# Differential attention: an odd key tile's value product first, the even one queued right behind it

## The chip, the cores and the metric

The kernel runs on one core of one Trainium2 chip. The metric is device time in microseconds (us) of one execution. A program of this kind has one instruction stream for each engine: TensorE (PE, its weight loads are listed as PEld), VectorE (DVE), ScalarE (ACT), GpSimd (POOL) and SyncE (SP, which issues most transfers). Each stream is worked off in its order, and the engines wait for one another by semaphores.

## The reference

A two-layer diffusion transformer block on 256 context tokens and 1024 latent tokens, width 1024. Each layer mixes tokens in three groups of heads (RWKV-7, differential attention, windowed attention), projects the result and runs a gated MLP. What the change touches is the differential attention: four heads, two softmax maps for each, and one product of their difference with the values.

```python
def diff_core(q, k, v, lam):
    s = jnp.einsum('bqhmd,bkhmd->bhmqk', q, k, preferred_element_type=F32) * (DF_QK ** -0.5)
    p = jax.nn.softmax(s, axis=-1)
    p = p[:, :, 0] - lam * p[:, :, 1]
    return jnp.einsum('bhqk,bkhd->bqhd', p.astype(v.dtype), v)
```

## The kernel before

`run` (line 2046) goes through the two layers. In a layer come, one after the other but overlapping at their borders: the input projection, token mixing, the output projection and the MLP. Token mixing is the RWKV scan (`rw_rest`, 20 steps, each a chain of small products) with the differential attention beside it, and then the windowed attention (`gq_units`, line 1439). All arithmetic is float32.

The differential attention (`df_units`, line 1299) is made of units, one for each head and group of query blocks: layer 0 has three groups for each head (256 context queries, then twice 512 latent queries), layer 1 the two latent ones. A unit has two generators. `scores` (line 1334) takes the scores once with the queries on the partitions, for their maxima and sums (lines 1356, 1369, 1371, 1349), and writes minus the maximum as further rows of the queries (`max_rows`, line 1207). `values` (line 1393) takes the scores again with a tile of 128 keys on the partitions, for each of the two maps (line 1412), exponentiates them into a tile `p` on ScalarE (line 1413), forms the difference of the maps in place on VectorE (line 1418), and multiplies by the values on TensorE (line 1425).

That value product has a stationary operand of 128 keys by 64 channels. Key tiles of even number add up in rows 0 to 63 of the accumulator `o`, those of odd number in rows 64 to 127; `result` (line 1400) copies `o` out on ScalarE (line 1402), adds the halves by a product with `fold` (line 1405) and finishes the head. A latent unit has ten key tiles, so five pairs; a context unit two, so one pair. That makes 84 pairs in all: 44 in layer 0 and 40 in layer 1. One product of 512 queries is two records in the trace (two passes over float32 operands).

Buffers that matter: `p` has three (`PTB`), the score banks `ds` in PSUM two (`XB`; the second scores, the first scores, the modulation's products `ada` and the folding share them), the accumulator `od` one (`ODB`), keys `ks` and values `vh` of a head one each.

What sets the order: the two products of a pair are emitted together by `product`, which is put on the list `late` and emitted one pair late (`flush`, `DLD`). `streams` (line 1234) interleaves the scores of later units with the values of earlier ones by their costs, and `blend` adds the modulation of the next half layer (`ada`, line 284). The emission order is only a priority. A planner then fixes the order of each engine's stream before the run, from its own estimate of when each instruction's operands are ready; the differential attention is emitted after the RWKV scan, with its priority raised over up to 4000 (layer 0) or 1000 (layer 1) earlier instructions (`HPO`). An even tile's `p` is ready before the odd tile's, and nothing ties the two products of a pair together in TensorE's stream.

Of the kernel before, what the change touches and what calls it, by code (L numbers as in the profile page):

```python
# [17 lines left out]
PSUM = bass.MemoryType.PSUM  # L18
DRAM = bass.MemoryType.DRAM

D = 1024
T = 1280
# [134 lines left out]
class K:  # L157
# [16 lines left out]
    def sbuf(self, name, tags=(), side="left"):  # L174
        """open an SBUF pool for these tags (all that have no pool of their own if none are given)"""
        es = ExitStack()
        p = es.enter_context(self.tc.tile_pool(name=name, bufs=1, reuse_waits="tile", side=side))
        for t in tags:
            self.pools[t] = p
            es.callback(self.pools.pop, t)  # L180
        if not tags:
            self.mp = p
        return es

    def psum(self, name, banks, side="left"):
        """open a PSUM pool; banks: use (None: any other) -> (tag, number of banks)"""
        es = ExitStack()
        self.pp = p = es.enter_context(self.tc.tile_pool(name=name, bufs=1, space=PSUM, reuse_waits="tile", side=side))
        for n, (t, k) in banks.items():
            self.banks[n] = (p, t, k)  # L190
            es.callback(self.banks.pop, n, None)
        return es
# [4 lines left out]
    def sm(self, shape, tag, bufs=2, dt=F32):  # L197
        """small tile that outlives a phase"""
# [13 lines left out]
    def rsqrt(self, y, ss, scale, eps, n, op1=ALU.add, tag="n"):  # L212
        """y = (ss*scale op1 eps)^-1/2 on [128, n]; Newton from a bit estimate."""
# [20 lines left out]
    def split(self, hi, lo, src, eh, el):  # L234
        """hi + lo = src exactly (both float32r)."""
# [17 lines left out]
    def consts(self):  # L253
# [7 lines left out]
        # split queries, keys (feature-major, hi and lo rows per head) and values (token-major)  # L261
# [9 lines left out]
        # silu(c), silu(c_ctx), feature-major  # L271
# [12 lines left out]
    def ada(self, l, chunks, bufs):  # L284
        """silu(c) @ ada_w + ada_b by chunks of 256 columns, gates times their norm_g -> DRAM; a chunk's quarters
        side by side in the array's column groups"""
# [28 lines left out]
    def ada_first(self):  # L315
        """shift and scale of layer 0's mixing, feature-major: as modT gives them"""
# [30 lines left out]
    def modT(self, l, part):  # L347
        """A = norm_g*(1+sc), SH, feature-major [128, 2(x, ctx), 8]."""
# [17 lines left out]
    def params(self, l):  # L366
        """per-channel parameters, feature-major"""
# [18 lines left out]
    def rw_consts(self, l):  # L386
# [8 lines left out]
        # lora weights, block-diagonal over the directions: rows of w_up, then of a_up  # L395
# [53 lines left out]
    def xsrc(self, i, t):  # L449
        """DRAM rows of token tile t of the stream after step i (i = -1: inputs)."""  # L450
# [9 lines left out]
    def norm_rows(self, src, tiles):  # L460
        """rows of these token tiles, normalized"""
# [20 lines left out]
    def norm_steps(self, src, tiles, A, SH, dst, one=None, hb=HB):  # L482
        """dst(k) -> (hi, lo) APs of the columns of these token tiles (only column `one` if given)."""
# [16 lines left out]
    # token tiles of the two halves of each group  # L500
# [15 lines left out]
    def wchunk(self, l, cols):  # L516
        """Split weight pieces of w_in[l] for the 8 row blocks; cols: [(first, width)]."""
# [17 lines left out]
    def fm_proj(self, W, o, m, evac, g, halves):  # L535
        """feature-major projection to columns o..o+m of chunk W over the tokens of group g's halves"""
# [8 lines left out]
    def rw_proj(self, W, o, j, g, halves):  # L545
        """raw projection of channel tile j (r0 r1 k0 k1 v0 v1) -> DRAM"""
# [25 lines left out]
    def tm_proj(self, W, i, j, w):  # L572
        """token-major projection of tile j of half i"""
# [6 lines left out]
    def rope(self, dst, ps, tab, g, dim):  # L580
        """dst = rope(ps), ps [128, g*dim]; tab [128, 2*dim] = cos | signed sin."""
# [16 lines left out]
    def parts(self, x, src, n, w, d, scale=1.0):  # L598
        """x [128, 2*w] = hi and lo values of scale*src's n groups of d columns, side by side per group"""
# [8 lines left out]
    def stacks(self, x, n):  # L608
        """[128, n, 128]: the n [128, 128] tiles of x transposed"""
# [14 lines left out]
    # (first output column, columns of w_in) of the chunks of the attention projections  # L624
    ATTN = ((0, [(960, 512)]), (512, [(1472, 256), (2240, 256)]), (1024, [(1728, 512)]))

    def attn_proj(self, l, g, W0=None, done=None):
        """q, k, v of both attentions (q and k split) -> DRAM"""
# [3 lines left out]
        for base, cols in self.ATTN:  # L632
            W = W0 if W0 and base == 0 else self.wchunk(l, cols)
            for i, j, t in [(i, j, t) for i in range(2) for j, t in enumerate(self.GROUPS[g][i])]:
# [28 lines left out]
                def store(base=base, t=t, x=x, tok=tok):  # L663
                    if base == 0:
                        st = self.stacks(x, 8).rearrange("p (a h) t -> p a h t", a=2)
                        # queries as high, high, low rows; keys as high, low, high rows
# [21 lines left out]
    def in_rwkv(self, l, g):  # L688
        """projections of the RWKV group"""
# [16 lines left out]
    def in_weights(self, l):  # L706
        """the first chunk's weights, in slots that the FFN is done with"""
# [14 lines left out]
    def in_first(self, l, src, done):  # L722
        """group 0"""
# [21 lines left out]
    # Both channel tiles (two heads each) run side by side. Index u of a step's matrices is  # L745
    # (direction, channel tile, head). Steps are prepared in batches; BATCH lists each batch's steps.
    BATCH = ((0, 1, 2, 3), (4, 5, 6, 7, 16, 17, 18, 19), (8, 9, 10, 11, 12, 13, 14, 15))

    def rw_conv(self, ct, pr, v, last, x):
        """width-3 convolution of r, k, v of one channel tile over 256 tokens; v goes to its tile"""  # L750
# [31 lines left out]
    def rw_prep(self, st, ct, pr, last, x=""):  # L782
        """Chunk operands of both directions for a 256-token piece of one channel tile (two heads).

        Direction 1 runs on reversed tokens: its storage index is T-1-token."""
# [16 lines left out]
        # normalised kk  # L802
# [7 lines left out]
        # decay: cumulative log decay of the chunk, inclusive and exclusive  # L810
# [20 lines left out]
        # in-context rate  # L831
# [56 lines left out]
    def chunk(d, s):  # L888
        """storage chunk of step s (context first in both directions)"""
        return s if d == 0 else (16 + s if s < 4 else s - 4)  # L890

    def rw_system(self, st, ct, b, p0):
        """the unit-triangular systems of four steps of batch b (from its position p0) -> DRAM"""
# [18 lines left out]
    def rw_inverse(self, b):  # L912
        """inverses of the batch's 32x32 diagonal blocks -> DRAM, as they are and transposed"""
# [24 lines left out]
    def rw_gram(self, st, s):  # L938
        """masked Gram matrices of step s; the systems' quadrant holds the inverses"""
# [33 lines left out]
    def rw_kv(self, st, s):  # L973
        """token-major keys (times the decay of the rest of the step) and values of step s"""
# [22 lines left out]
    def rw_step(self, st, s, last):  # L997
# [7 lines left out]
        # rows 0..63: outputs, rows 64..127: right sides of the systems  # L1005
# [59 lines left out]
    def rw_readout(self, st, tiles, tag="rt", bufs=6, end=False):  # L1065
        """group norm, bonus, output gate of two token tiles -> scr_y"""
# [43 lines left out]
    def sooner(self, g, offset):  # L1110
        """a generator whose instructions go before up to `offset` earlier ones"""
# [8 lines left out]
    def together(*gs):  # L1120
        """run generators side by side"""
# [9 lines left out]
    def beside(*gs):  # L1131
        """one generator that runs these side by side"""
# [12 lines left out]
    def rw_first(self, l, last):  # L1145
        """what the first steps need"""
# [46 lines left out]
    # Scores are taken twice: with queries on the partitions, for their maxima, and with keys on the  # L1193
    # partitions and minus the maximum as further rows of the product, for the exponentials, which are
    # then the moving operand of the product with [V | 1].
# [3 lines left out]
    def cast(self, out, in_):  # L1199
        """load split values (exact)"""  # L1200
        self.nc.gpsimd.dma_start(out=out, in_=in_)

    def ones(self, k, r):
        """the rows of the keys that meet the maxima"""
        self.nc.gpsimd.memset(k[r:r + 8].bitcast(F32), 1.0)

    def max_rows(self, q, r, nm, n, mask, bank="mT"):
        """rows r..r+8 of q [128, n*128]: for column block b, nm[:, b]'s high part in row b and low part in row 4+b"""
# [12 lines left out]
    def unflip(self, o, n, d, tag, bank="yT"):  # L1221
        """[128 rows, n, d] PSUM view of o [d, n*128] PSUM, transposed"""
# [11 lines left out]
    def streams(self, units, late, lead, ahead):  # L1234
        """units: (scores, values, their costs), generators that yield costs; the values run beside the scores of
        up to `lead` units further on, both streams at the same share of their total costs. A unit's last entry is the
        number of units whose values have to be done before its scores. Yields costs too."""
# [22 lines left out]
    def blend(*gs):  # L1260
        """run generators (with their total costs) side by side, at the same share of the costs"""
# [10 lines left out]
    def limit(g, cost):  # L1272
        """the part of a generator up to a cost"""
# [8 lines left out]
    def flush(late, n):  # L1282
        """emit the products with the values but for the latest n"""
# [3 lines left out]
    def neg_log(self, y, L, n):  # L1287
        """y = -ln(L) on [128, n] for L >= 1: estimate from the bits, then Newton steps on exp"""
# [10 lines left out]
    def df_units(self, l, late):  # L1299
        """differential attention: units of a head for up to four row blocks"""  # L1300
# [5 lines left out]
        for hd in range(DF_HEADS):  # L1306
# [23 lines left out]
            for gi, (t0, nt) in enumerate(groups):  # L1330
# [3 lines left out]
                def scores(t0=t0, nt=nt, nk=nk, us=us, hs=hs, first=gi == 0, head=head, hd=hd):  # L1334
# [7 lines left out]
                    # maxima and sums of the context keys (0) and of the other keys (1)  # L1342
# [4 lines left out]
                    def chunk(c, m, i, s):  # L1347
                        """exponentials' sum of chunk c, component m, row block i"""
# [44 lines left out]
                def values(t0=t0, nt=nt, nk=nk, us=us, hs=hs, finish=finish):  # L1393
# [14 lines left out]
                    for j in range(nk):  # L1408
# [13 lines left out]
                        def product(pair=tuple(pair)):  # L1422
                            for j, p in pair:
                                r = 64 * (j % 2)
                                mm(o[r:r + 64, :w], v[:, j], p[:, 0, :w], start=j < 2, stop=j >= nk - 2)
# [13 lines left out]
    def gq_units(self, l, late):  # L1439
        """windowed attention: units of the four heads of a key group at one row block"""  # L1440
# [5 lines left out]
        for qt, g in ((qt, g) for qt in range(t1, NT) for g in range(2)):  # L1446
# [23 lines left out]
            def scores(g=g, qt=qt, kts=kts, us=us, hs=hs, head=head):  # L1470
# [14 lines left out]
                def prod(o, h, k0, n):  # L1485
                    """scores of head h against n keys from tile k0"""
# [75 lines left out]
    def post(self, y, ss, rs, gate, x, out, junk):  # L1562
        """out = x + y*rsqrt(mean y^2)*gate for y given as two [128, 512] halves"""
# [589 lines left out]
```

## Time and profile before

| | us |
|---|---|
| median of 3 runs | 4740.43 |
| lowest and highest run | 4727.01, 4759.02 |
| span of the profiled execution | 4717.0 |
| TensorE busy in it | 4264.7 (90%) |
| VectorE, GpSimd, ScalarE busy | 3238.9 (69%), 2324.3 (49%), 1861.2 (39%) |

The span runs from the first to the last instruction of one profiled execution, a separate one from the three timed runs. Its own time outside the span is not recorded, so the three runs are the only whole times. Busy time of TensorE counts from the start of a product to its modelled end, so products that follow each other closely overlap in it.

The value products stand in eight stretches of the span, four for each layer (one for each head): 556 to 628, 768 to 823, 964 to 1032 and 1201 to 1301 us in layer 0; 2975 to 3036, 3156 to 3200, 3344 to 3391 and 3555 to 3636 us in layer 1. The last stretch of each layer lies beside the windowed attention, the others beside the RWKV scan.

### The profile page before, as it was taken

What the parts mean: (1) busy time and instruction counts of PE and PEld (TensorE: products, weight loads), DVE (VectorE), ACT (ScalarE), POOL (GpSimd) and SP (SyncE); (2) the same over time, 40 slices, a digit from 0 to 9 for tenths busy, and PEclk for the clock granted to TensorE, in tenths of its full rate; (3) what the DMA queues carried; (4) which work ended last, traced back from release to release, by engine and by line L of the source; (5) the groups of instructions that cost most, each with busy time, mean ns of one, the idle gap of its engine ahead of it and who ended that gap; (6) DMA issues with size and microseconds to landing.
All of it is one profiled execution on the core that took longest, in us unless ns stands there. A gap on an engine that the chain in (4) does not pass through costs nothing. (4 is left out here: it accounts for less than half of the span.)

```text
span 4717.0 us, 71390 instructions
## 1 busy us (share of the span) xinstructions
PE 4264.7 (90%) x25999; PEld 3353.6 (71%) x25999; DVE 3238.9 (69%) x6313; ACT 1861.2 (39%) x3692; POOL 2324.3 (49%) x2295
## 2 busy tenths in 40 slices
PE   8997998989998999889988989889899989897897
PEld 5885664845567899779977866457555678886886
DVE  4347666777756877887774366656776478888887
ACT  3334544534333333433333344555443233333332
POOL 3336225243445666576654252542534366667664
PEclk9996868977999999999999985789879889998998
DMA  7453223251132222232235461222510322223222
GB/s 211 127 144 94 63 71 95 60 149 57 29 128 94 87 83 83 88 113 81 81 106 163 121 149 27 72 56 68 130 49 29 114 95 90 85 90 99 86 89 85
DMA packets 500637, 441.20 MB, mean 94 GB/s; under 512 B 120372, under 2 KB 432828, under 8 KB 500286
## 3 DMA queue, kind: packets, MB, share of 16 engines
q1 hardware_dynamic: 447070, 381.44, 27.1%
q0 software_dynamic: 21056, 51.26, 4.1%
q10 hardware_dynamic: 32160, 3.94, 0.5%
q8 instruction: 205, 3.36, 0.3%
q14 instruction: 146, 1.20, 0.1%
HBM read 353.02 MB, written 83.51 MB: 93 GB/s over the span
## 5 line engine op out<-in xcount | busy, mean ns | idle before, releaser
L244 DVE TENSOR_TENSOR wl<-wraw,fwh 128x1024 fp32r<-128x1024 f32 x176 | 324.1, 1842 | 160.4 <-ACT fwh L238 159.8
L238 ACT ACTIVATE fwh<-wraw 128x1024 fp32r<-128x1024 f32 x264 | 272.2, 1053 | 301.7 <-DVE wraw L1854 169.0
L248 PE MATMUL m<-h,fwh 128*128 128x322 f32 (+1 forms) x1056 | 320.7, 304 | 15.4 <-ACT fu L1900 8.6
L248 PE MATMUL dn<-dh,ahl 128*128 128x512 f32 x792 | 315.9, 403 | 14.9 <-ACT ahl L238 9.3
L244 POOL TENSOR_TENSOR gp<-gx,gp 128x512 fp32r<-128x512 f32 x160 | 207.5, 1301 | 246.0 <-DVE gp L240 166.8
L249 PE MATMUL dn<-dl,ahl 128*128 128x512 f32 x792 | 319.4, 403 | 8.6 <-POOL dl L244 8.6
L250 PE MATMUL m<-h,wl 128*128 128x322 f32 (+1 forms) x1056 | 318.6, 302 | 4.3 <-DVE wl L244 4.3
L249 PE MATMUL m<-h,fwh 128*128 128x322 f32 (+1 forms) x1056 | 321.0, 304 | 0.0
L244 POOL TENSOR_TENSOR dl<-dr,dh 128x1024 fp32r<-128x1024 f32 x88 | 218.8, 2486 | 200.1 <-ACT dh L238 197.8
L250 PE MATMUL dn<-dh,ahl 128*128 128x512 f32 x792 | 305.4, 400 | 0.0
L1349 ACT ACTIVATE ds<-ds,dnm 128x512 f32<-128x512 f32 (+1 forms) x400 | 232.3, 581 | 185.0 <-DVE dnm L1371 106.9
L248 PE MATMUL m<-T,fwh 128*128 128x322 f32 (+1 forms) x704 | 222.2, 316 | 88.2 <-DVE fraw L1871 76.3
L244 POOL TENSOR_TENSOR wl<-wraw,fwh 128x1024 fp32r<-128x1024 f32 x88 | 230.1, 2615 | 123.0 <-ACT fwh L238 118.8
L1413 ACT ACTIVATE p<-ds 128x512 f32<-128x512 f32 (+1 forms) x336 | 187.4, 585 | 234.2 <-PE ds L1412 201.5
L1962 DVE TENSOR_TENSOR yacc<-dn,yacc 128x512 f32<-128x512 f32 x360 | 231.0, 680 | 26.4 <-PE dn L250 26.3
L244 POOL TENSOR_TENSOR ahl<-cv,ahl 128x642 fp32r<-128x642 f32 (+1 forms) x88 | 131.8, 1498 | 233.0 <-ACT ahl L238 214.0
L1930 ACT ACTIVATE cv<-cv 128x642 f32<-128x642 f32 (+1 forms) x88 | 60.5, 687 | 467.6 <-DVE cv L1929 467.6
L1371 DVE TENSOR_REDUCE dnm<-ds 128x1 f32<-128x512 f32 x256 | 173.9, 686 | 87.6 <-PE ds L1369 86.1
L244 DVE TENSOR_TENSOR wl<-wr,wh 128x512 fp32r<-128x512 f32 (+1 forms) x76 | 66.6, 879 | 239.5 <-ACT wh L238 136.7
L250 PE MATMUL m<-T,wl 128*128 128x322 f32 (+1 forms) x704 | 217.1, 308 | 8.6 <-DVE wl L244 8.6
L249 PE MATMUL m<-T,fwh 128*128 128x322 f32 (+1 forms) x704 | 218.7, 311 | 1.3 <-DVE T L244 1.2
L248 PEld LDWEIGHTS m<-h,fwh 128*128 128x128 f32 x1056 | 205.0, 194 | 19.9 <-ACT fu L1900 9.8
(499 smaller groups left out, 13524.0 us busy)
## 6 DMA issues: line engine op xcount, KB each, us to landing
wraw<-in_ff_w_gate_dram SPq DMA_DIRECT2D x88, 512.0 KB
wraw<-in_ff_w_up_dram SPq DMA_DIRECT2D x88, 512.0 KB
dr<-in_ff_w_down_dram SPq DMA_DIRECT2D x88, 512.0 KB
aw<-in_ada_w_dram SPq DMA_DIRECT2D x160, 256.0 KB
wr<-in_w_in_dram SPq DMA_DIRECT2D x88, 256.0 KB
x<-scr_x SPq DMA_DIRECT2D x28, 512.0 KB
scr_df<-st SPq DMA_DIRECT2D x80, 128.0 KB
scr_gq<-st SPq DMA_DIRECT2D x18, 512.0 KB
```

Of the source, the lines that this page charges most:

```text
L238: nc.scalar.activation(hi, src, AF.Copy)
L244: e.tensor_tensor(out=lo, in0=src, in1=hi, op=ALU.subtract)
L248: mm(out, lh, rh, start=first, stop=False)
L249: mm(out, lh, rl, start=False, stop=False)
L250: mm(out, ll, rh, start=False, stop=last)
L1349: act.activation(s, s, AF.Exp, bias=nm[:, c, m, i:i + 1], accum_out=L[:, c, m, i:i + 1])
L1371: vv.tensor_reduce(out=nm[:, 1 + c, m, i:i + 1], in_=s, axis=AX.X, op=ALU.max, negate=True)
L1413: act.activation(p[:, m, :w], s[:, :w], AF.Exp)
L1930: act.activation(t[:, m], t[:, m], AF.Silu)
L1962: vv.tensor_tensor(out=ys[i][:, hs], in0=ps, in1=ys[i][:, hs], op=ALU.add)
```

## The change

Inside `product`, the odd tile's product is emitted first. The even tile's product follows inside `issue_after`, which adds an edge without a semaphore: in TensorE's own stream the even product may only stand behind the odd one. The rows of `o` that each writes, the operands, and the first and last flags stay as they were.

```diff
                         def product(pair=tuple(pair)):
-                            for j, p in pair:
-                                r = 64 * (j % 2)
-                                mm(o[r:r + 64, :w], v[:, j], p[:, 0, :w], start=j < 2, stop=j >= nk - 2)
+
+                            (j0, p0), (j1, p1) = pair
+                            i1 = mm(o[64:128, :w], v[:, j1], p1[:, 0, :w], start=j1 < 2, stop=j1 >= nk - 2)
+                            with self.tc.issue_after(i1.ins):
+                                mm(o[0:64, :w], v[:, j0], p0[:, 0, :w], start=j0 < 2, stop=j0 >= nk - 2)
+                            j = j1
                             if j == nk - 1:
                                 result()
```

The rest of the diff removes comments and docstrings.

## Rows read from the trace of the kernel before

**Rows 1.** The page: the span, and TensorE's busy time, share and instructions.

```profile
span 4717.0 us, 71390 instructions
PE 4264.7 (90%) x25999; PEld 3353.6 (71%) x25999; DVE 3238.9 (69%) x6313; ACT 1861.2 (39%) x3692; POOL 2324.3 (49%) x2295
```

**Rows 2.** Busy time by stretch: line 1425 alone, TensorE and its weight loads, clock.

```profile
556.00:628.00 72.00, 27.65 (x44) 4.62 (x44) 0.82 0.28 80
768.00:823.00 55.00, 21.84 (x44) 4.03 (x44) 0.93 0.45 132
964.00:1032.00 68.00, 22.62 (x44) 4.05 (x44) 0.80 0.67 171
1201.00:1301.00 100.00, 22.10 (x44) 4.02 (x44) 1.00 0.11 29
2975.00:3036.00 61.00, 25.44 (x40) 4.49 (x40) 0.81 0.28 77
3156.00:3200.00 44.00, 23.10 (x40) 4.19 (x40) 0.90 0.36 104
3344.00:3391.00 47.00, 20.14 (x40) 3.73 (x40) 0.96 0.54 139
3555.00:3636.00 81.00, 20.16 (x40) 3.72 (x40) 1.00 0.08 23
sum 528.00, PE 183.04 PEld 32.85; mean PE 22.88 PEld 4.11
```

**Rows 3.** TensorE's timeline: products of line 1425 by themselves (start, length, idle before).

```profile
560.85 1.07 PE L1425 MATMUL od<-p,vh 128*64 128x512 f32 x2
...
585.44 1.97 PE L1425 MATMUL od<-p,vh 128*64 128x512 f32 x2
...
780.48 1.07 PE L1425 MATMUL od<-p,vh 128*64 128x512 f32 x2
781.48 0.73 PE L1412 MATMUL ds<-qs,ks 104*128 104x512 f32 x2
782.14 1.07 PE L1425 MATMUL od<-p,vh 128*64 128x512 f32 x2
...
3634.81 1.07 PE L1425 MATMUL od<-p,vh 128*64 128x512 f32 x2
```

**Rows 4.** The same timeline: two products of a pair side by side, x4.

```profile
625.06 1.97 PE L1425 MATMUL od<-p,vh 128*64 128x512 f32 x4
...
990.86 1.08 PE L1425 MATMUL od<-p,vh 128*64 128x512 f32 x4
```

**Rows 5.** Line 1425 by itself: its weight loads (shortest, median, longest in ns).

```profile
L1425 PEld LDWEIGHTS od<-p,vh x336: 132/136/232, 556.1 to 3634.9; 128*64 128x64 f32 x168
```

**Rows 6.** All engines by stretch: TensorE, weight loads, VectorE, ScalarE, GpSimd, clock.

```profile
556.00:628.00 72.00, 65.62 (x397) 31.03 (x398) 61.51 (x192) 36.04 (x70) 19.71 (x27) 0.82 0.28 80
768.00:823.00 55.00, 49.41 (x430) 22.45 (x431) 29.90 (x70) 26.19 (x48) 39.30 (x65) 0.93 0.45 132
1201.00:1301.00 100.00, 100.00 (x359) 52.02 (x359) 71.31 (x174) 38.72 (x75) 43.69 (x43) 1.00 0.11 29
3555.00:3636.00 81.00, 79.54 (x283) 40.26 (x283) 54.77 (x121) 32.85 (x63) 31.64 (x30) 1.00 0.08 23
```

**Rows 7.** The timeline at 813 us: the next RWKV step's first weight load on TensorE.

```profile
813.55 0.57 PEld L962 LDWEIGHTS off<-XT,G 32*32 32x32 f32 x16 [0.81 <-DMA XT<-scr_i]
```

**Rows 8.** ScalarE's and VectorE's timelines: a tile's two exponentials, its difference.

```profile
782.01 1.09 ACT L1413 ACTIVATE p<-ds 128x512 f32<-128x512 f32 x2 [0.58 <-PE ds L1412]
...
780.98 0.75 DVE L1418 SCALAR_TENSOR_TENSOR p<-p,ls 128x512 f32<-128x512 f32 x1 [1.42 <-ACT p L1413]
```

**Rows 9.** Who waited for line 1425 (us in total, times).

```profile
  ACT p L1413: 28.6, 8
```

**Rows 10.** All engines by stretch, columns as in rows 6: two stretches of RWKV steps.

```profile
642.60:690.40 47.80, 47.80 (x260) 38.49 (x256) 22.38 (x49) 18.18 (x48) 9.07 (x17) 0.50 0.06 16
813.00:953.20 140.20, 138.20 (x1598) 115.64 (x1597) 97.39 (x222) 77.08 (x211) 45.59 (x76) 1.00 0.28 70
```

## The prediction, made blind

> **What bounds the kernel now.** I read the page first: TensorE is busy 90% of the span, VectorE 69%, the others less [rows 1]. So work taken off TensorE can shorten the run, where TensorE is what ends last. The second view is line 1425 by stretch: the value products fill 183.04 us of TensorE's busy time, in eight stretches of 528 us together [rows 2]. That sum is the ceiling of anything that the change can touch.
>
> The third view is TensorE's timeline, and it shows what the change is about. A product by itself (x2, its two passes) takes 1.07 us at full clock and 1.97 at half; from its start at 780.48 to the next instruction at 781.48 it holds TensorE for 1.00 us [rows 3]. Where the two products of a pair happen to stand side by side (x4), both together take 1.08 us at full clock and 1.97 at half [rows 4]. The second one is free: it uses the other 64 columns of the array at the same time. Read through the whole timeline, the x2 row stands 130 times (first and last in [rows 3]), x4 13 times, and 4 times x6, which is a pair and a third product alone. That is 134 products alone, or 67 pairs apart, and 17 together, of 84. By stretch, in order of time, the pairs apart are 9 of 11, 9 of 11, 6 of 11, 10 of 11 in layer 0 and 8, 9, 7, 9 of 10 in layer 1.
>
> The fourth view is all engines by stretch, for the question whether TensorE is the one that ends last. Beside the windowed attention it is: busy 100.00 of 100 us and 79.54 of 81, with VectorE at 71.31 and 54.77 [rows 6]. In the stretch at 556 it is busy 65.62 of 72, but VectorE 61.51 [rows 6]; the one at 2975 is like it. In the stretch at 768 GpSimd is busy 39.30 of 55, TensorE 49.41 [rows 6], and the stretch ends with a weight load of the next RWKV step that waits for a transfer, XT<-scr_i [rows 7], which brings the inverse that GpSimd works out. The one at 3156 is like that.
>
> **The change, part by part.** No instruction is added or removed, and no transfer moves. The even product moves later in TensorE's stream, to just behind the odd one.
>
> *Packing.* A pair apart costs 2 x 1.00 us, packed 1.01 or so: half goes. Per stretch that is line 1425's busy time [rows 2] x share of pairs apart x 1/2:
>
> - 1201 and 3555 us: 22.10 x 10/11 / 2 = 10.0 and 20.16 x 9/10 / 2 = 9.1, together 19.1. TensorE ends last there, so all of it is on the path.
> - 556 and 2975 us: 27.65 x 9/11 / 2 = 11.3 and 25.44 x 8/10 / 2 = 10.2, together 21.5. VectorE is late next: it leaves 72 - 61.51 = 10.5 us in the first. Between none and all I take half, 10.8, since VectorE can't be filled to the last us.
> - 964 and 3344 us: 22.62 x 6/11 / 2 = 6.2 and 20.14 x 7/10 / 2 = 7.0, together 13.2. These end in the RWKV read-out, with transfers beside it. Half again, 6.6.
> - 768 and 3156 us: 21.84 x 9/11 / 2 = 8.9 and 23.10 x 9/10 / 2 = 10.4, together 19.3. The RWKV step waits for the inverse and its transfer whatever TensorE does [rows 7]. I take 0; the cover is GpSimd's chain, and if the freed time is filled with later work all 19.3 could come.
>
> Sum: 19.1 + 10.8 + 6.6 + 0 = 36.5 us. Bounds: 19.1 (the first line alone) and 73.1 (all).
>
> The row says that the second product of a pair costs 0.01 us more than none [rows 3, 4]. [...]
>
> *The new wait.* The even product now waits for the odd tile's `p`, and with it the even tile's buffer is freed one tile later. `p` has three buffers, so the tile after next needs the pair's product. Its loop is: products 1.07 [rows 4], two exponentials 1.09, difference 0.75 [rows 8], 2.91 us, with three hand-overs about 3.0 (an estimate). Today two tiles take 2 x (782.14 - 780.48) = 3.32 us where nothing else stands between [rows 3]. So the new wait does not lengthen the densest pace, but it eats two thirds of the 1.00 us saved there. This is a second reason for the 0 in the last line above. Beside the windowed attention a pair has 81 to 100 us for ten or eleven, some 8 to 9 us each, so the loop decides nothing. Below nothing: ScalarE already waits 28.6 us, 8 times, for the products [rows 9]; doubling that is the loss that this wait could bring if the planner's order doesn't fill TensorE meanwhile. Queued behind the waiting odd product on TensorE are the next scores and the modulation's products, and the banks that these need are freed by exponentials that wait for `p`.
>
> *The order elsewhere.* The planner sees other ready times, so other instructions of token mixing move too. The trace of before can't price that; I put it in the range, within the bounds above.
>
> The profiled execution has a span of 4717.0 us [rows 1]; 36.5 less is 4680.5. The median of the runs is 23.4 above that span, and the same edit to it gives 4703.9.
>
> **The rivals.**
>
> *All of it comes.* TensorE's chain is dense on both sides of every stretch, and time freed while RWKV waits is filled with later scores. For it: 138.20 busy of 140.20 us right behind the stretch at 768 [rows 10]. Against: VectorE's 61.51 of 72, and the inverse. 4740.4 - 73.1 = 4667.3.
>
> *The buffers of `p` take the place.* Outside the windowed attention the stretches keep their length. For it: the loop of 3.0 against 3.32. Against: at half clock a pair apart takes 2 x 1.97, which is more than the loop. 4740.4 - 19.1 = 4721.3.
>
> *It doesn't do what it says.* Another ready instruction gets between the two, or the packing needs the even product first, as it stands today. Then nothing is saved and the even product only waits. Against: an instruction tied to one just issued is ready at once, and the two halves of the array are alike. About 4740.
>
> *Slower, through the clock.* RWKV steps ran from 813 at a granted clock of 1.00 for 140.2 us, and from 642.6 at 0.50 for 47.8 us, TensorE busy all the time in both [rows 10]. The clock that these small products get is the one that they find: the dense stretch before 813 had 0.93, the one before 642.6 had 0.82 [rows 6]. If packed pairs leave TensorE idle in the dense stretches, the steps at 813 (and their like in layer 1) start at half. 47.8 us at half would be 23.9 at full, so two such stretches cost 47.8; with only the 19.1 gained, 4740.4 + 47.8 - 19.1 = 4769.1. It decides where the granted clock at 813 is 0.50; beyond 133 us at half in the two together it passes 1%. Against: the stretch at 768 had 0.93 although TensorE was idle for 5.6 of its 55 us [rows 6], so a little more idle time need not tip it. [...]
>
> **How the numbers follow.** Chances: forecast 0.46, all 0.22, buffers 0.13, nothing 0.06, clock 0.13. One per cent, about what a measurement of this kernel can tell from no change, is 47.4 us: 4693.0 and 4787.8. Faster by more: the second case, and that part of the forecast where the halves come nearly whole (4740.4 - 19.1 - 21.5 - 13.2 = 4686.6), 0.14: 0.36. Slower by more: the clock case where half clock lasts longer, and a little of the new wait: 0.10. Within: 0.54. The range runs from 4660, a little under "all", to 4770, the clock case; beyond lie perhaps 0.06 below and 0.08 above.
>
> **What would show it.** Right: nearly all rows of line 1425 are x4 with 1.08 or 1.97, its busy time is near 183.04 - 73.1 = 110 us, and the stretches beside the windowed attention are 9 to 10 us shorter with TensorE still full. The steps after 813 start no earlier. Wrong: x2 rows remain; or line 1425's busy time halves and the stretches keep their length, with ScalarE's wait for line 1425 grown far over 28.6 us; or a granted clock of 0.50 in the RWKV steps that had 1.00.

## The result and the profile after

The change made the kernel slower: 4767.84 us median of 20 runs (4738.81 to 4823.12) against 4743.91 of 20 runs of the kernel before, ratio 1.0073, 95% interval 1.0047 to 1.0098. The forecast was 4704.

The pages, the kernel after; its counterpart is [rows 1].

```profile
span 4753.5 us, 71339 instructions
PE 4285.9 (90%) x25999; PEld 3402.8 (72%) x25999; DVE 3225.7 (68%) x6313; ACT 1861.1 (39%) x3692; POOL 2323.0 (49%) x2295
```

The span is 36.5 us longer. TensorE does the same products and is busy 21.2 us more, while every other engine is busy as long as before or a little less.

TensorE's timeline after, around one pair (start, length, line, operands), in answer to [rows 3, 4]:

```profile
574.37 0.64 PE L1425 MATMUL od<-p,vh 128*64 128x512 f32 x1
574.37 0.64 PE L1427 MATMUL od<-p,vh 128*64 128x512 f32 x1
574.85 0.59 PE L1425 MATMUL od<-p,vh 128*64 128x512 f32 x1
574.85 0.59 PE L1427 MATMUL od<-p,vh 128*64 128x512 f32 x1
575.37 0.50 PE L1412 MATMUL ds<-qs,ks 104*128 104x512 f32 x1
```

Odd (L1425) and even (L1427) start together in both passes, and the pair holds TensorE from 574.37 to 575.37, 1.00 us. Of 84 pairs 83 stand so, their products at most 0.04 us apart; in the one left (at 566.46) another product comes between. Line 1427's time by stretch, which is the pairs' time (columns as in [rows 2]):

```profile
562.00:630.00 68.00, 16.47 (x22) 2.69 (x22) 0.71 0.32 87
771.00:833.00 62.00, 13.67 (x22) 2.43 (x22) 0.81 0.39 113
981.00:1043.00 62.00, 17.22 (x22) 2.78 (x22) 0.69 0.73 167
1203.00:1293.00 90.00, 11.37 (x22) 2.10 (x22) 1.00 0.13 33
2983.00:3040.00 57.00, 16.70 (x20) 2.58 (x20) 0.67 0.26 73
3175.00:3222.00 47.00, 16.01 (x20) 2.42 (x20) 0.72 0.35 96
3373.00:3430.00 57.00, 14.54 (x20) 2.29 (x20) 0.82 0.60 149
3602.00:3672.00 70.00, 10.72 (x20) 1.91 (x20) 1.00 0.09 27
sum 513.00, PE 116.69 PEld 19.21; mean PE 14.59 PEld 2.40
```

The products fell from 183.04 to 116.69 us, so packing did its work. But read the third-last column, the granted clock: in the six stretches beside the RWKV scan it was 0.82, 0.93, 0.80, 0.81, 0.90, 0.96 before and is 0.71, 0.81, 0.69, 0.67, 0.72, 0.82 now. In the two beside the windowed attention it is 1.00 in both kernels.

Where the span went, all engines by stretch (columns as in [rows 6]). First the kernel before: head 0's first product to head 3's first, head 3's products, for each layer.

```profile
556.10:1201.10 645.00, 584.71 (x4476) 377.67 (x4475) 458.02 (x1191) 305.24 (x745) 247.06 (x357) 0.82 0.31 83
1201.10:1301.40 100.30, 100.30 (x360) 52.25 (x360) 71.58 (x177) 39.10 (x76) 43.59 (x43) 1.00 0.11 29
...
2975.90:3555.40 579.50, 527.64 (x3828) 335.77 (x3827) 393.33 (x937) 283.59 (x680) 264.06 (x387) 0.83 0.29 74
3555.40:3636.30 80.90, 79.44 (x283) 40.29 (x283) 54.46 (x121) 33.15 (x63) 31.93 (x31) 1.00 0.08 23
```

The same stretches after:

```profile
562.00:1203.20 641.20, 578.04 (x4428) 386.80 (x4427) 443.53 (x1172) 301.79 (x739) 242.28 (x352) 0.76 0.32 83
1203.20:1293.20 90.00, 89.78 (x367) 51.65 (x367) 69.09 (x174) 39.60 (x78) 45.21 (x44) 1.00 0.13 33
...
2983.00:3602.80 619.80, 552.86 (x3830) 362.51 (x3829) 390.79 (x936) 283.10 (x680) 262.41 (x387) 0.74 0.27 69
3602.80:3672.40 69.60, 67.65 (x277) 37.88 (x277) 50.00 (x120) 31.88 (x62) 30.81 (x28) 1.00 0.09 27
```

Beside the windowed attention 10.3 and 11.3 us were gained. The RWKV part of layer 0 got 3.8 us shorter, that of layer 1 40.3 us longer, with the clock down from 0.83 to 0.74. The stretch between the layers' value products took 15.3 us more and the start 5.9: in all -10.3 - 11.3 - 3.8 + 40.3 + 15.3 + 5.9 + 0.4 (the rest) = 36.5.

The 40 us of layer 1 are spread over its three RWKV parts. From one head's first product to the next head's, before and then after:

```profile
2975.90:3156.60 180.70, 156.16 (x1137) 98.57 (x1136) 125.55 (x283) 99.44 (x235) 94.04 (x154) 0.77 0.23 60
3156.60:3344.70 188.10, 184.54 (x1888) 135.56 (x1888) 117.96 (x266) 96.80 (x237) 73.73 (x111) 0.96 0.28 72
3344.70:3555.40 210.70, 186.94 (x808) 101.65 (x807) 149.82 (x389) 87.35 (x208) 96.29 (x123) 0.77 0.34 86
```

```profile
2983.00:3175.90 192.90, 164.36 (x1135) 109.54 (x1134) 117.50 (x282) 98.23 (x235) 88.40 (x151) 0.69 0.22 56
3175.90:3373.10 197.20, 186.50 (x1770) 138.41 (x1770) 115.60 (x249) 95.16 (x232) 73.03 (x111) 0.84 0.26 65
3373.10:3602.80 229.70, 202.00 (x926) 114.55 (x925) 157.70 (x405) 89.71 (x213) 100.98 (x126) 0.71 0.32 83
```

These are 12.2, 9.1 and 19.0 us more. In layer 0 the same three parts changed by -3.0, +14.0 and -14.8 us, and the clock fell in each of them too (0.72, 0.97, 0.78 before; 0.67, 0.87, 0.74 after). So a lower clock did not make every part longer.

One piece of it close up: the RWKV steps behind head 1's stretch in layer 1 ran from 3188.9 to 3332.3 at 1.00 before. After, the first third of them is at half clock:

```profile
3204.90:3256.10 51.20, 47.21 (x277) 30.79 (x278) 17.63 (x43) 19.33 (x43) 14.13 (x24) 0.50 0.40 88
3256.10:3361.90 105.80, 105.00 (x1220) 89.01 (x1220) 74.28 (x157) 57.56 (x156) 29.37 (x48) 1.00 0.20 49
```

TensorE is busy 47.21 of 51.20 us there and issues 277 products, 5.4 for each us; in the row below 11.5. Who waited for the products, the kernel after (lines 1425 and 1427), in answer to [rows 9]:

```profile
  ACT p L1413: 21.1, 10
...
  ACT p L1413: 76.1, 34
```

ScalarE's wait for a free `p` grew from 28.6 to 97.2 us, as the new wait would have it. So two suspects stand side by side, the clock and the wait, and a third: the planner gave all of token mixing another order.

### The profile page after: what moved, and what is told of

Read it like the earlier page. It is cut to its first block, busy times and chain, and to the rows that moved or that the text cites. A ratio compares the mean times of both kernels' runs of the same rounds, so it can differ in the third digit from the quotient of the medians.

```text
span 4753.5 us, 71339 instructions
## 1 busy us (share of the span) xinstructions
PE 4285.9 (90%) x25999; PEld 3402.8 (72%) x25999; DVE 3225.7 (68%) x6313; ACT 1861.1 (39%) x3692; POOL 2323.0 (49%) x2295
## 5 line engine op out<-in xcount | busy, mean ns | idle before, releaser
L244 POOL TENSOR_TENSOR wl<-wr,wh 128x512 fp32r<-128x512 f32 (+1 forms) x76 | 99.7, 1312 | 245.9 <-ACT wh L238 176.8
```

Source lines behind the costliest of these rows:

```text
L244: e.tensor_tensor(out=lo, in0=src, in1=hi, op=ALU.subtract)
```

## The experiments

Theory A: packing lowers the granted clock where RWKV steps lie beside and behind, and that takes back more than it saves. Theory B: the wait for `p` stretches the values. Theory C: any other order from the planner moves the clock, and with it the time, as much. Ratios are to the kernel before, timed in the same series (its medians in the five series: 4730 to 4757 us), with 95% intervals. `...` marks what a code cut leaves out.

**same_cols**: the changed order, not packed.

```diff
-i1 = mm(o[64:128, :w], v[:, j1], p1[:, 0, :w], start=j1 < 2, stop=j1 >= nk - 2)
+i1 = mm(o[0:64, :w], v[:, j1], p1[:, 0, :w], start=j1 < 2, stop=False)
...
-    mm(o[0:64, :w], v[:, j0], p0[:, 0, :w], start=j0 < 2, stop=j0 >= nk - 2)
+    mm(o[0:64, :w], v[:, j0], p0[:, 0, :w], start=False, stop=j0 >= nk - 2)
```

`result` then copies and folds 64 rows.

> Both products of a pair go to the same 64 columns and add up in one half of the accumulator, in the changed order: the odd one first, the even one tied behind it. So the order and the new wait on the odd tile stay, the packing is undone (a pair takes about 2.0 us of TensorE at full clock instead of 1.01). Theory A (the clock: packing takes dense streaming off TensorE, so the RWKV steps behind it start at half clock) expects the granted clock back at about 0.89 over the span, the steps behind the second head at 1.00, and a time of 0.998 to 1.004 of the kernel before. Theory B (the wait: the even product is held, the tiles p come free two at a time, and the stretches stretch) expects 1.007 or more, since the wait is all there and the packing gain is gone.

Measured 0.9955 (0.9926 to 0.9983): faster than both, and better than A's range from 0.998 on. Timeline of a pair, and ScalarE's wait for it:

```profile
786.04 1.07 PE L1425 MATMUL od<-p,vh 128*64 128x512 f32 x2
786.95 1.02 PE L1427 MATMUL od<-p,vh 128*64 128x512 f32 x2
```

```profile
  ACT p L1413: 75.2, 33
```

The two products follow each other, nothing is packed, and the wait is still 75.2 us. Theory B falls: with most of its wait in place the kernel was faster. The mean clock went to 0.894 (0.892 before, 0.868 after).

**head3** and **heads012**: the change for head 3 alone (`hd == 3`), and for heads 0 to 2 alone; the others as before.

```diff
+if not (hd == 3):    # heads012: hd < 3
+    for j, p in pair:
+        r = 64 * (j % 2)
+        mm(o[r:r + 64, :w], v[:, j], p[:, 0, :w], start=j < 2, stop=j >= nk - 2)
+    ...
```

> The change only for the last head of each layer, whose products lie beside the windowed attention; heads 0 to 2 as before. Theories A and B both expect the gain of the two stretches beside the windowed attention, 9 to 10 us each by the profile, and none of the loss: about 4744 - 19 = 4725, a ratio of 0.996 (0.993 to 0.999). If the loss comes from a reordering of token mixing as a whole (theory C), it could come out anywhere from 0.993 to 1.007.

> The change for heads 0 to 2 of each layer, head 3 as before. The counterpart of head3, which measured 0.9972. If the parts add up, the loss of heads 0 to 2 alone is 1.0073 - 0.9972: 1.009 to 1.012, with a granted clock over the span of 0.87 or less. Theory C expects no such sum: anything from 0.997 to 1.010.

Measured 0.9972 (0.9948 to 0.9996) and 1.0002 (0.9967 to 1.0038). head3 is as both theories said. heads012 is a miss: the parts give 0.997 together, not 1.0073. That they don't add up speaks for C.

**swap_only**: the odd product first, the tie left out.

```diff
-i1 = mm(o[64:128, :w], ...)
-with self.tc.issue_after(i1.ins):
-    mm(o[0:64, :w], ...)
+mm(o[64:128, :w], ...)
+mm(o[0:64, :w], ...)
```

> The odd product is emitted first, but nothing ties the even one behind it, so the planner is free to put the even one as early as before. Theories A and B expect 1.000 (0.998 to 1.002), with most products of a pair apart again (x2 rows). Theory C (any small change of the order moves the time this much) expects a difference of 0.4% or more, either way.

Measured 1.0048 (1.0014 to 1.0082), but the expectation rested on a wrong premise. Every engine's instructions stand in the trace in the same order as the change's; only two overlapping records of line 1216 have changed places. So with the odd product emitted first the tie moves nothing, and this is a repeat of the change. As such it is of use, since one program was profiled twice (the change, then swap_only):

```profile
core 0: 4753.5 us, clock 0.868
```

```profile
core 0: 4777.1 us, clock 0.863
```

In the traces of before and after the granted clock stands at 1.00 or 0.50 and nowhere between (73 and 80 stretches at each), so the time at half clock is 2 x (1 - clock) x span: 1254 and 1307 us by the trace (1021.5 in the kernel before). With no instruction moved, 53 us more at half clock go with 23.6 us more of span, 0.44 us each. The timed executions, which have their span and mean clock on record, bear this price out: within each of the 19 programs other than the kernel before, whose executions differ in no instruction, the span rises by 0.29 to 0.43 us with each us at half clock (correlation 0.91 or more), and within each of the five series of the kernel before by 0.35 to 0.43.

The repeat also shows how roughly one execution tells a stretch. Layer 1's RWKV part took 635.4 us here (619.8 in the change's first profile), and the two stretches beside the windowed attention were not at full clock:

```profile
1195.70:1292.80 97.10, 96.86 (x367) 55.36 (x367) 68.02 (x173) 39.59 (x78) 44.55 (x44) 0.91 0.12 31
3627.50:3699.50 72.00, 70.05 (x275) 39.15 (x275) 49.98 (x120) 31.48 (x62) 30.39 (x28) 0.95 0.10 26
```

They gained 3.2 and 8.9 us on the kernel before, 12.1 in place of 21.6.

**filler**: the change, and behind each pair of heads 0 to 2 a product with zero weights over all 128 columns. **kick**: ten such products, only behind head 1's last pair in each layer.

```diff
 with self.tc.issue_after(i1.ins):
     mm(o[0:64, :w], ...)
+    if hd < 3:    # kick: head 1's last pair, ten times
+        mm(o[0:128, :w], self.zer, p0[:, 0, :w], start=False, stop=j0 >= nk - 2)
 ...
```

> The change, and in heads 0 to 2 one further product behind each pair, with weights of zero over all 128 columns (two passes, about 0.86 us at full clock; it adds zeros to the accumulator). That puts nearly all the TensorE time back that packing saves there, and keeps the order, the wait and the packing. Theory A expects the granted clock in the first three stretches of each layer back up to 0.80 to 0.93, the RWKV steps behind the second head at 1.00, and with the 19 us gained beside the windowed attention a ratio of 0.994 to 1.001. Theory B expects it as slow as the change or slower, 1.007 to 1.015, since TensorE has more to do and the wait is longer by the filler.

> The change, and ten products with weights of zero over all 128 columns (0.86 us each at full clock, 8.6 us) behind the very last pair of head 1 in each layer, just ahead of the RWKV steps. Theory A in the form 'the steps run at the clock that they find' expects the granted clock at their start at 1.00 and the 51 us of half clock behind head 1 in layer 1 gone: 1.0073 less about 20 us, plus what of the 17 us of filler isn't hidden, 1.000 to 1.006. If the clock of the steps doesn't depend on what stands just ahead of them, it stays slow and the filler adds: 1.007 to 1.011.

The 0.86 us of these expectations is what the trace of before shows for two passes of 512 columns at clock 1.00: 20 passes of line 332, one behind the other (from 16.83), take 8.74 us, 0.87 for two.

filler measured 1.0001 (0.9973 to 1.0030): with more work on TensorE than the change, and the same wait (ScalarE waits 97.3 us), it is not slower but level with the kernel before, clock 0.884. That is as A expected and against B; but the planner gave it another order too, so that the added work did it is not shown. kick measured 1.0122 (1.0064 to 1.0181), a miss for A's sharper form. Its trace in layer 0 (the filler runs from 865.9 to 877):

```profile
400.00:590.00 190.00, 159.30 (x1004) 120.25 (x1004) 103.02 (x248) 84.20 (x219) 77.69 (x150) 0.50 0.27 65
860.00:870.00 10.00, 8.07 (x16) 2.63 (x13) 1.81 (x3) 2.51 (x5) 8.28 (x18) 0.67 0.94 220
870.00:881.00 11.00, 9.90 (x46) 5.18 (x45) 2.13 (x5) 3.17 (x6) 1.60 (x3) 0.97 0.53 141
881.00:911.00 30.00, 30.00 (x230) 24.06 (x229) 14.22 (x45) 12.14 (x39) 6.62 (x14) 0.50 0.17 47
911.00:1050.00 139.00, 136.89 (x1613) 110.79 (x1615) 103.51 (x225) 72.75 (x186) 41.73 (x64) 1.00 0.22 59
```

The clock came up while the filler ran (0.67 in the row in which it starts, 0.97 in the next) and fell again 4 us after its end, with TensorE busy 9.90 of 11.00 us, and stayed at half for 30 us in which TensorE was busy all the time. So the RWKV steps did not simply keep the clock that they found. And the first row, where no value product has run yet, was at 0.50 for all its 190 us, against 0.68 in the change:

```profile
400.00:590.00 190.00, 153.40 (x1218) 109.82 (x1216) 133.32 (x330) 99.78 (x253) 88.70 (x162) 0.68 0.31 75
```

Nothing of what is tested lies there; only the planner's order differs. The repeat of the change's order (swap_only) has 0.68 in this stretch again. That is theory C at work.

**h1_cols**: the change, head 1 not packed (`r1` is 0 for `hd == 1`, 64 else). **combo**: heads 0 to 2 not packed, head 3 packed (`hd < 3`).

```diff
-i1 = mm(o[64:128, :w], ...)
+i1 = mm(o[r1:r1 + 64, :w], ...)
```

The flags and `result` follow for the heads that are not packed, as in same_cols.

> The change, but head 1 not packed (same 64 columns, same order and tie). In the profile of the change the loss of layer 1 arises behind head 1's stretch, where the RWKV steps run at half clock for 51 us, and part of layer 0's too. Theory A in the form that it is this start which costs expects the steps behind head 1 at 1.00 and 0.995 to 1.001. If the clock loss is spread over all three heads' stretches, it expects 1.001 to 1.005, some third to half of the loss gone. Theory B expects 1.005 or more.

> Heads 0 to 2 as in same_cols (changed order, both products of a pair in the same 64 columns, so not packed); head 3, beside the windowed attention, packed as in the change. Theory A (packing costs where RWKV steps follow and pays beside the windowed attention, where the clock is 1.00 anyway) expects the two to add up: 0.9955 less the 10 to 20 us of the last stretches, 0.992 to 0.995 of the kernel before, the fastest so far. Theory B (wait) expects no more than head 3 alone, 0.997. Theory C (the planner's order decides, whatever is packed) expects anything between 0.993 and 1.005.

h1_cols measured 0.9971 (0.9937 to 1.0004): with one head's 21 pairs not packed, and another order, the whole loss is gone. Its expectation put layer 1's loss behind head 1; only 9.1 of the 40.3 us lie there. combo measured 0.9904 (0.9863 to 0.9944), 4708.54 us against 4757.23 of the kernel before beside it, the fastest, and a little faster than A's 0.992 to 0.995 and C's 0.993 and up. Its profiled execution has a clock of 0.902, at the upper end of its timed ones (median 0.894). In this first order the median clock of the timed executions goes with the number of heads 0 to 2 that are packed: 0.894 for none (same_cols, combo), 0.881 for two (h1_cols), 0.877 and 0.867 for three (heads012, the change).

**Other orders.** Two parameters of emission that change no work gave three more orders: d is AHD 0.3 to 0.2, e ADS 4 to 6, h ADS 4 to 3, each in the kernel before, the change, and combo; same_cols in d too.

```diff
-AHD = (0.3, 0.3)
+AHD = (0.2, 0.2)    # e: ADS = (6, 6); h: ADS = (3, 3)
```

> The kernel before with the values' stream starting earlier against the scores (AHD 0.2 for 0.3), which gives the planner another order of token mixing and changes no work. It is the base of a first other order, for after_d and combo_d. Theory C (the order alone moves the time as much as the change did, through the clock) expects it 0.5% or more from the kernel before, either way. Theory A (packing is what costs) expects it within 0.4%.

> The change, with AHD 0.2. Theory A expects it slower than before_d by about what the change cost in the first order, 0.4 to 1.0%. Theory C expects no fixed sign against before_d.

> combo (packed for head 3 alone, heads 0 to 2 in the same columns) with AHD 0.2. Theory A expects it faster than before_d by 0.3 to 1.0% and faster than after_d by 1.0 to 1.8%. Theory C expects a difference from after_d of either sign.

> same_cols (nothing packed, changed order with the tie) with AHD 0.2; before_d measured 1.0053, after_d 1.0060, combo_d 0.9957. If queueing the two products behind each other without packing is what helps against the kernel before (0.9955 in the first order), it is 0.3 to 0.7% faster than before_d, 0.998 to 1.002. If that first gain was luck of one order, it is level with before_d, 1.003 to 1.008.

> The kernel before with the modulation's products spread otherwise (ADS 6 for 4): a second other order, the base for after_e and combo_e. Theory C expects it 0.5% or more from the kernel before, either way; theory A within 0.4%.

> The change, with ADS 6 for 4; its base is before_e, which measured 1.009 of the kernel before. Packing as a cost in every order (theory A) expects it slower than before_e by 0.4 to 1.0%, 1.013 to 1.019. Order alone (theory C) expects either sign: in order d the change was 1.0060 against its base's 1.0053, no difference.

> combo with ADS 6 for 4. If unpacked heads 0 to 2 help in every order, it is faster than after_e by 1.0 to 1.6% (as in the first two orders: 0.9904 against 1.0073, 0.9957 against 1.0060) and its granted clock is higher by 0.015 or more. Theory C expects a smaller difference or one of the other sign.

> The kernel before with ADS 3 for 4, a third other order. Theory C, which the orders d and e bear out (1.0053 and 1.009), expects 0.5% or more from the kernel before; now rather slower than faster.

> The change, with ADS 3 for 4. Theory A expects it slower than before_h by 0.4 to 1.0%; theory C either sign.

> combo with ADS 3 for 4; before_h measured 1.0044 and after_h 1.0074 of the kernel before. In the first three orders combo was 0.97, 0.96 and 1.17% faster than its base and 1.7, 1.0 and 0.4% faster than the change. Theory A expects the same sign again against after_h, 0.991 to 1.001, and a granted clock over 0.885. Theory C, as a full explanation, expects 1.002 or more as often as not.

| order | before | the change | same_cols | combo |
|---|---|---|---|---|
| as given | 1 | 1.0073 (1.0047 to 1.0098) | 0.9955 (0.9926 to 0.9983) | 0.9904 (0.9863 to 0.9944) |
| d | 1.0053 (1.0009 to 1.0097) | 1.0060 (1.0018 to 1.0101) | 1.0007 (0.9978 to 1.0037) | 0.9957 (0.9915 to 0.9999) |
| e | 1.0090 (1.0051 to 1.0128) | 1.0011 (0.9980 to 1.0042) | | 0.9973 (0.9940 to 1.0006) |
| h | 1.0044 (1.0018 to 1.0070) | 1.0074 (1.0046 to 1.0103) | | 0.9960 (0.9929 to 0.9990) |

And from the profiled executions: mean clock / us at half clock / us of value products.

| order | before | the change | same_cols | combo |
|---|---|---|---|---|
| as given | 0.892 / 1021 / 183 | 0.868 / 1254 / 117 | 0.894 / 1002 / 186 | 0.902 / 919 / 166 |
| d | 0.886 / 1084 / 194 | 0.866 / 1277 / 131 | 0.890 / 1046 / 204 | 0.890 / 1042 / 183 |
| e | 0.875 / 1203 / 187 | 0.876 / 1172 / 118 | | 0.896 / 981 / 178 |
| h | 0.889 / 1052 / 181 | 0.869 / 1252 / 121 | | 0.894 / 999 / 163 |

Three readings; each quotient of two ratios is uncertain by 0.3 to 0.6%, from the two intervals. The change against its base (the kernel before in the same order): +0.73, +0.07, -0.78, +0.30%. The first and the third are clear of their uncertainty and have opposite signs, so being slower than before is a matter of the order that the planner happened to give; A had expected 0.4 to 1.0% slower in each. The base itself moved 0.4 to 0.9% with the order, as C said (0.5% or more; h falls a little short). But combo against the change is faster in all four, by 1.7, 1.0, 0.4 and 1.1%: in three clearly, in e within the uncertainty and short of the 1.0 to 1.6% expected. The profiled executions have 191 to 335 us less at half clock, and the median clock of the timed ones is higher in each order (0.894 to 0.867, 0.890 to 0.868, 0.887 to 0.875, 0.892 to 0.870). So packed heads 0 to 2 went with a lower clock in every order tried, as A said. The two kernels do not have the same order, so it is shown that the clock goes with the packing, not how. And combo against its base is 0.96, 0.95, 1.16 and 0.84% faster, the one gain that held in each.

Over the 18 profiled executions without filler products, a least-squares fit of the span to two numbers of each trace gives: span = 4246 us + 0.35 x (us at half clock) + 0.59 x (us of value products), with 6.4 us left over where the spans scatter by 31 (standard deviations). Its price of half clock agrees with the 0.29 to 0.43 found within single programs. For the change that is 0.59 x (117.4 - 183.0) = -39 and 0.35 x (1254 - 1021.5) = +82, together +43; measured +36.5.

## Why the prediction was wrong

*Packing*: right. 83 of 84 pairs are together, the products fell by 66.4 us (183.04 to 116.69) where 73.1 was worked out. What is missing goes with the clock: of 320 records with 512 columns 124 take over 0.8 us, 59 before. The count of 17 pairs together before was three too many: in three of those rows the two products run one behind the other (at 3029.83 and 3387.26) or half overlap (at 978.22). That would put some 3 us on the 73.1 and changes nothing in the outcome.

*The first line of the sum*, 19.1 us beside the windowed attention: right in the profile of the change, 10.3 + 11.3 = 21.6, at clock 1.00 in both kernels; the repeat, at 0.91 and 0.95, gained 12.1. In whole times head3 bears a gain out (0.28%, 0.04 to 0.52), and combo against same_cols points the same way (0.51% in the first order, 0.50% in d, each about as large as its uncertainty).

*The halves and the zero* (10.8, 6.6, 0): as a price for freed TensorE time the whole sum was near, since the fit gives 39 us where I had 36.5. The halves were guesses, so that is in part luck. Stretch by stretch it can't be told, because the clock moved in the same stretches.

*The step that failed* is that the sum had no term for the clock. I had the mechanism as a rival at 0.13, with 4769.1, and dismissed it with "the stretch at 768 had 0.93 although TensorE was idle for 5.6 of its 55 us [rows 6], so a little more idle time need not tip it". That stretch went to 0.81, and five others fell likewise. In the place of the term that was missing the runs show 232 us more at half clock, some 82 us of span by the fit, against the 39 that the products saved. The measured 4767.84 next to the rival's 4769.1 is luck: the two places that it named, behind head 1, paid 14.0 and 9.1 us for its 23.9 each, and the steps there were at half clock from the start in layer 1 alone. The rest of the loss came elsewhere in layer 1 (12.2 and 19.0 us) and between the layers (15.3), and the last RWKV part of layer 0 got 14.8 us shorter. Its reason, that the steps run at the clock that they find, fell with kick.

*The order elsewhere*: failed. I held it to "within the bounds above", as if it were small change. Three orders of the same work made the kernel before slower by 21 to 43 us (0.44 to 0.90% of 4744), about as much as the whole forecast gain.

*The new wait*: right that the waiting grows, but it more than tripled (97.2 us, 28.6 before) where a doubling was allowed for; and right that it does not set the pace, since same_cols keeps 75.2 us of it and is faster than before. The three hand-overs in its loop of 3.0 us, an estimate, are 0.03 us (product to exponential, after), 0.03 (exponential to difference) and 0.05 (difference to product, both before), medians by the traces. *It doesn't do what it says*: out, though the tie adds nothing to emitting the odd product first; odd and even products are equally long after (379/643/1117 ns for lines 1425 and 1427 alike: shortest, median, longest). *All of it comes* and *the buffers of `p` take the place*: out, both had the kernel faster.

What stays open: the planner gave each variant its own order, and no run here has the change's order without its packing. So it isn't settled why the same work in another order, or packed, is granted a lower clock. Nor is it settled why queueing the two products unpacked (same_cols) was 0.45% faster than its base in the first order, and as much in d, there within the uncertainty.

## What to carry to other kernels

Where TensorE's granted clock switches between 1.00 and 0.50, as here, price a saving on TensorE together with the time at half clock: here 66 us of products came off and 232 us more ran at half speed. Pack where TensorE is full and the clock at or near 1.00 (beside the windowed attention: 22 us gained in one execution, 12 in another) and leave the products unpacked where the clock switches (beside the RWKV scan, 0.67 to 0.82 with packing, 0.80 to 0.96 before); combo, made so with the two products of a pair queued, was about 1% faster than its base in four orders. And before a difference under 1% is put down to an edit of an instruction stream that a planner reorders, time the kernel before in a few other orders.

## What was not expected of the hardware

One program, profiled twice, spent 1254 and 1307 us at half clock and 4753.5 and 4777.1 us in all. In kick the clock, 0.97 from 870 to 881, was 0.50 for the next 30 us, of which TensorE's rows show it busy for 30.00, and 1.00 for the 139 behind them. More work did not cost time here: with filler's 63 products with zeros, all on TensorE and on top of the change, and the order that came with them, the ratio was 1.0001 and not 1.0073.
